# Running streams of a hybrid encoder: cached latents loaded in both layouts, and the two streams of a pair in turn

## The chip, the core and the metric

The kernel runs on one core of a Trainium2 chip. The metric is the device time of one execution in microseconds (us). TensorE (PE) multiplies, VectorE (DVE) and ScalarE (ACT) read its results from PSUM, GpSimd (POOL) works on SBUF alone, and SyncE (SP) issues the DMA transfers, in the order of its own program.

## The reference, cut to what matters

One layer of an encoder with two attention branches side by side, for a prompt of 2048 new tokens and for 8 running streams with 16 new tokens each and 2048 cached positions. The change touches the second branch (latent heads, MLA) of the running streams only:

```python
def mla_attention(q_lat, q_pe, q_pos, ckv, kpe, k_pos):
    mask = chunk_mask(q_pos, k_pos)
    s = (jnp.einsum('bqhc,bkc->bhqk', q_lat, ckv)
         + jnp.einsum('bqhr,bkr->bhqk', q_pe, kpe)).astype(jnp.float32) * MLA_SCALE
    p = masked_softmax(s, mask)
    return jnp.einsum('bhqk,bkc->bqhc', p.astype(ckv.dtype), ckv)
```

`ckv` is the cache of latents, 2048 positions by 256 (fp32) for each stream; `kpe` the positional keys, 2048 by 64. The latents are used twice: contracted over their 256 dimensions for the scores, and over the positions for the output. There are 4 heads, so one stream has 64 rows of queries. The other branch of the running streams is differential attention over cached keys and values of 128 dimensions per head, 4 heads, two softmaxes each.

## The kernel before

The program has four stages: the projections (`_phase_a`, `_phase_a2`), the prompt's attention (`_phase_b`), the running streams (`_sample`), and the output projections with the final norm (`_phase_c`). A scheduler orders the instructions of each engine beforehand, by priorities that follow the program and by its own timeline; on the chip every engine then keeps that order and waits on semaphores.

`_gates` makes tanh factors from a projection of the tokens: for a group of 384 tokens 16 units of 24 matmuls each (L98 to L100, tile `z`), with one weight tile of 512 KB loaded (L380), split on ACT and DVE (L112, L113), and the result stored (L388, L389). The units of groups 3 and 4 may be issued only after the prompt's attention, so they fill PE between the parts of the running streams.

`_sample` works through pairs of streams: `diff_stream(b)`, `mla_streams(b)`, `diff_stream(b + 1)`. A differential stream loads 4 tiles of keys (L734) and 4 of values (L769), 1 MB each; its four heads' scores (L737) go to partitions 0, 32, 64 and 96 of one PSUM bank. `mla_streams` treats two streams at once: stream x writes partitions 64x to 64x + 63 of a bank, its 64 rows. It runs in four chunks of 512 keys. In `chunk(i)` the latents come as [128 positions, 8, 256] (L804, every other chunk, one tile of 1 MB per stream). For each stream PE transposes 2 x 4 blocks of 128 x 128 against the identity (L809), ACT and DVE copy them to a tile `kT` (L816, L814), and then three matmuls follow: two with the latents (L819) and one with the positional keys (L822), where stream x uses rows 64x to 64x + 63 of both operands. The softmax's maximum and exponential are at L716 and L717. After the fourth chunk the weights are scaled on POOL (L846) and transposed (L857), and the output is made in two halves of 1024 keys: eight matmuls for stream 0, then eight for stream 1 (L861), from the same tiles of latents.

All of the big tiles, keys, values, latents and positional keys, come out of one ring (`pk`, tag `k`) of 8 buffers of 1 MB; a load waits until the tile 8 places ahead of it has been read. A second ring `pkt` holds the `kT`. All loads and stores are issued by SP.

`_phase_c` loads the heads' outputs (`ox`, L1175), multiplies them with norm factors on POOL (`r`, L1181), splits them, and multiplies (tile `y`). Its tiles take the memory that the gates' tiles held.

```python
    for b in range(0, NB, 2):
        diff_stream(b)
        mla_streams(b)
        diff_stream(b + 1)
```

Of the kernel before, what the change touches and what calls it, by code (L numbers as in the profile page):

```python
# [11 lines left out]
F32 = mybir.dt.float32  # L12
# [5 lines left out]
PSUM = bass.MemoryType.PSUM  # L18
DRAM = bass.MemoryType.DRAM

P = 128
# [94 lines left out]
def _outer(c, stack):  # L116
    """Pools for the work that fills the engines' gaps: the projections of the gates, later the output projections."""
# [9 lines left out]
def _phase_a(c):  # L127
    nc, tc = c.nc, c.tc
    with (
# [141 lines left out]
        def first_units(us):  # L271
            # the factors of a group follow the sums of the next one
# [14 lines left out]
        def kpe_block():  # L287
            # 64 columns: the weights' two parts side by side, their products added after the load in the next phase
# [61 lines left out]
def _gates(c, prio, g, after, ready):  # L350
    """tanh(m / 2) of m_a and m_b for one group of tokens; ready: the parts of the weights come from memory."""
# [40 lines left out]
def _phase_a2(c):  # L392
    nc, tc = c.nc, c.tc
    with (
# [168 lines left out]
        # the factors of the next group lie between two parts of this one's products  # L563
# [15 lines left out]
def _lam(c, pool, psum):  # L579
    # every partition: exp(sum lq1 lk1) - exp(sum lq2 lk2) + lam_init, negated  # L580
# [12 lines left out]
def _sample_prep(c, temp, psum):  # L593
    """Rotated queries and keys of the new tokens, step by step: rows (s, d); the latent heads' queries in the latent space."""
# [56 lines left out]
    # both halves of the partitions: the streams of a pair take one each  # L651
# [8 lines left out]
    nc.gpsimd.tensor_copy(x.rearrange("p (b h q) -> p b h q", b=NB, h=H), zp.rearrange("p (h b q) -> p b h q", h=H, b=NB))  # L660
# [10 lines left out]
def _sample(c, stack):  # L671
    """Attention of the running streams."""
    nc, tc = c.nc, c.tc
    pkt = stack.enter_context(tc.tile_pool(name="s_kt", bufs=4, reuse_waits="tile"))
    p1 = stack.enter_context(tc.tile_pool(name="s_1", bufs=1, reuse_waits="tile"))
    pk = stack.enter_context(tc.tile_pool(name="s_k", bufs=8, reuse_waits="tile"))
# [21 lines left out]
    # row (h, s, q) of a batch belongs to column (h, q); the second map has weight -lam  # L698
# [9 lines left out]
    def softmax(scores, nm):  # L708
        # scores: PSUM views [128, n]; exponentials (two tiles of 1024 keys, the new keys) and their factors
# [9 lines left out]
        # pm holds the negated maxima  # L719
# [72 lines left out]
    def mla_streams(b):  # L792
# [4 lines left out]
        ks = {}  # L797

        def chunk(i):
            ps = bank("s", f"s{nm}_{i}")  # L800
            for x in range(2):
                if i % 2 == 0:
                    ks[x, i // 2] = big([P, 8, 256], f"k{nm}_{i}_{x}")
                    nc.sync.dma_start(ks[x, i // 2], c.i["cc"][b + x][:, 4 * i : 4 * i + 8, :])  # L804
                kT = pkt.tile([P, 2, 512], F32, tag="kT", name=f"kT{nm}_{i}_{x}", bufs=4)
                for ct in range(2):
                    pk_ = bank("pt", f"kt{nm}_{i}_{x}_{ct}")
                    for j in range(4):
                        nc.tensor.transpose(  # L809
                            pk_[:, j * P : (j + 1) * P],  # L810
                            ks[x, i // 2][:, 4 * (i % 2) + j, ct * P : (ct + 1) * P], c.ident,
                        )
                    if ct:
                        nc.vector.tensor_copy(kT[:, ct], pk_)  # L814
                    else:
                        nc.scalar.copy(kT[:, ct], pk_)  # L816
                out = slice(64 * x, 64 * x + 64)
                for ct in range(2):
                    nc.tensor.matmul(  # L819
                        ps[out, :], QL[:, ct, b + x].rearrange("p h q -> p (h q)"), kT[:, ct], start=(ct == 0), stop=False  # L820
                    )
                nc.tensor.matmul(  # L822
                    ps[out, :], QP[out, b + x].rearrange("p h q -> p (h q)"), kpe[out, i * 512 : (i + 1) * 512],
                    start=False, stop=True,
                )
            return ps

        def fresh():
            ps = bank("pt", f"sn{nm}")
            for x in range(2):  # L830
                bc = slice((b + x) * QS, (b + x + 1) * QS)
                out = slice(64 * x, 64 * x + 64)
                for ct in range(2):
                    nc.tensor.matmul(
                        ps[out, :QS], QL[:, ct, b + x].rearrange("p h q -> p (h q)"), cnT[:, ct, bc], start=(ct == 0), stop=False
                    )
                nc.tensor.matmul(ps[out, :QS], QP[out, b + x].rearrange("p h q -> p (h q)"), kpn[out, bc], start=False, stop=True)
# [5 lines left out]
        for i, e in enumerate(es):  # L843
# [15 lines left out]
            for x in range(2):  # L859
                for kt in range(8):  # L860
                    nc.tensor.matmul(  # L861
                        po[64 * x : 64 * x + 64, :256], at[:, kt * P + 64 * x : kt * P + 64 * x + 64], ks[x, i][:, kt, :],
# [22 lines left out]
    # factors of the sub-norm of the prompt's heads and queries  # L885
# [22 lines left out]
def _phase_b(c):  # L908
    nc, tc = c.nc, c.tc
    GQ = 256  # L910
    with (
# [21 lines left out]
        class Chunks:  # L933
            """Keys [128, 512] or values [128, 4, 128] of one head, loaded 512 keys at a time."""
# [15 lines left out]
        def load_q2(name, src, cols):  # L950
            # src [2 (hi, lo), 64, T]: both halves of the partitions get the same rows
# [411 lines left out]
```

## Time and profile before

| | us |
|---|---|
| runs | 2703.49, 2713.54, 2716.29 |
| median | 2713.54 |
| profiled execution, first to last instruction | 2710.0 |
| PE busy in it | 2569.4 |
| stretch of the running streams, first keys issued to last values issued | 1850.22 to 2267.72 |

The rows are those of one profiled execution of 2710.0 us; no time outside of this span is shown for it, so it is set beside the median of the runs as it stands. A busy PE counts a matmul until its modelled end, which reaches into the next one; what an instruction costs in a row of instructions is therefore read from start to start. An fp32 matmul stands in the trace as two instructions, a transpose as one.

### The profile page before, as it was taken

To read this page: it belongs to the slowest core of one execution; us is meant where nothing else is said; L and a number is where in the kernel's file an instruction comes from. 1 tells how busy PE (TensorE), PEld (TensorE's weight loads), DVE (VectorE), ACT (ScalarE), POOL (GpSimd) and SP (SyncE) were. 2 spreads that over 40 slices of the span, in tenths; PEclk is the share of its full clock that TensorE was granted. 3 is DMA by queue.
4 is the path that set the end of the run, shared out by engine and by line. 5 is a ranking of instruction groups with operands and counts; after the bars stand their busy time and mean duration, and the time that the engine had idled before them with its cause. 6 is when DMAs were issued, how large, how long until landed. Compare 5 with 4: busy or idle time off the path is not lost. (4 is left out here: it accounts for less than half of the span.)

```text
span 2710.0 us, 44913 instructions
## 1 busy us (share of the span) xinstructions
PE 2569.4 (95%) x16308; PEld 2267.0 (84%) x16308; DVE 1436.4 (53%) x3038; ACT 1067.8 (39%) x2682; POOL 703.5 (26%) x944
## 2 busy tenths in 40 slices
PE   7999999999888889999999999999999999999998
PEld 7999999999778878988988888877566575888887
DVE  8236752233666467868776677892323222533334
ACT  5111223212343366766655666772323222311111
POOL 7102220001344233344333334442001001122211
PEclk9999999999889999999999999999999999999999
DMA  5346777322677873474565667317659576534332
GB/s 183 115 147 207 266 255 225 121 68 92 204 243 230 263 218 117 126 202 148 165 194 173 223 203 224 99 54 316 236 220 345 188 291 203 192 117 128 113 108 99
DMA packets 291372, 496.17 MB, mean 183 GB/s; under 512 B 27440, under 2 KB 229200, under 8 KB 280144
## 3 DMA queue, kind: packets, MB, share of 16 engines
q1 hardware_dynamic: 291152, 493.31, 55.5%
q8 instruction: 129, 2.11, 0.3%
q14 instruction: 91, 0.75, 0.1%
HBM read 351.55 MB, written 141.66 MB: 182 GB/s over the span
## 5 line engine op out<-in xcount | busy, mean ns | idle before, releaser
L98 PE MATMUL z<-z_hi,zw 128*128 128x384 f32 (+1 forms) x768 | 262.9, 342 | 26.2 <-ACT zt L388 21.1
L100 PE MATMUL z<-z_hi,zw 128*128 128x384 f32 (+1 forms) x768 | 256.3, 334 | 2.1 <-DMA zw<-wz 1.9
L99 PE MATMUL z<-z_lo,zw 128*128 128x384 f32 (+1 forms) x768 | 257.3, 335 | 0.6 <-POOL z_lo L370 0.6
L977 DVE TENSOR_REDUCE pmd<-sd 128x1 f32<-128x512 f32 (+3 forms) x320 | 189.7, 603 | 58.5 <-PE sd L1051 30.4
L979 ACT ACTIVATE ed<-sd,pmd 128x512 f32<-128x512 f32 (+3 forms) x320 | 200.6, 631 | 47.6 <-DVE pmd L977 35.6
L1078 PE MATMUL sd<-k,q 128*128 128x512 f32 (+2 forms) x640 | 191.0, 384 | 3.5 <-ACT ed L979 1.5
L1018 POOL TENSOR_SCALAR ed<-ed,ad 128x512 f32<-128x512 f32 (+3 forms) x160 | 117.0, 747 | 278.1 <-DVE ad L994 120.5
L98 PEld LDWEIGHTS z<-z_hi,zw 128*128 128x128 f32 x768 | 147.5, 192 | 44.6 <-ACT zt L388 25.4
L99 PEld LDWEIGHTS z<-z_lo,zw 128*128 128x128 f32 x768 | 147.7, 192 | 7.3 <-issue 4.7
L100 PEld LDWEIGHTS z<-z_hi,zw 128*128 128x128 f32 x768 | 146.9, 191 | 6.6 <-DMA zw<-wz 2.3
L1018 POOL TENSOR_SCALAR em<-em,am 128x512 f32<-128x512 f32 (+3 forms) x160 | 104.3, 668 | 157.2 <-DVE am L994 97.1
L98 PE MATMUL y<-o,wh_ab 128*128 128x384 f32 (+1 forms) x384 | 129.0, 336 | 14.9 <-DVE sm L1197 14.9
L113 DVE TENSOR_TENSOR zw<-zs,zw 128x512 fp32r<-128x512 f32 x128 | 89.9, 728 | 92.7 <-ACT zw L112 92.3
L370 POOL TENSOR_TENSOR z_lo<-zx,z_hi 128x384 fp32r<-128x384 f32 (+1 forms) x48 | 48.0, 1026 | 334.6 <-DVE gt L260 260.5
L98 PE MATMUL ps_u<-hi,wh_u 128*128 128x384 f32 (+1 forms) x384 | 126.0, 328 | 6.5 <-ACT wh_u L112 6.5
L100 PE MATMUL y<-o,wl_ab 128*128 128x384 f32 (+1 forms) x384 | 127.8, 333 | 1.4 <-DVE wl_ab L113 1.4
L99 PE MATMUL y<-o,wh_ab 128*128 128x384 f32 (+1 forms) x384 | 128.2, 334 | 0.4 <-DVE o L113 0.4
L1202 ACT ACTIVATE m<-sm 128x384 fp32r<-128x384 f32 (+1 forms) x48 | 24.4, 508 | 259.5 <-POOL sm L1200 259.5
L98 PE MATMUL ps_z<-hi,wh_z 128*128 128x384 f32 (+1 forms) x384 | 125.1, 326 | 1.0 <-ACT wh_z L112 1.0
L99 PE MATMUL ps_u<-lo,wh_u 128*128 128x384 f32 (+1 forms) x384 | 125.7, 327 | 0.0
L99 PE MATMUL ps_z<-lo,wh_z 128*128 128x384 f32 (+1 forms) x384 | 125.0, 325 | 0.0
L100 PE MATMUL ps_u<-hi,wl_u 128*128 128x384 f32 (+1 forms) x384 | 124.9, 327 | 0.0
(365 smaller groups left out, 7567.2 us busy)
## 6 DMA issues: line engine op xcount, KB each, us to landing
zs<-in_wu_dram SPq DMA_DIRECT2D x64, 512.0 KB
zw<-wz SPq DMA_DIRECT2D x64, 512.0 KB
ksd<-in_ckT_dram SPq DMA_DIRECT2D x32, 1024.0 KB
vsd<-in_cv_dram SPq DMA_DIRECT2D x32, 1024.0 KB
q<-Qs SPq DMA_DIRECT2D x128, 128.0 KB
ksm<-in_cc_dram SPq DMA_DIRECT2D x16, 1024.0 KB
smT<-zt SPq DMA_DIRECT2D x80, 192.0 KB
sm<-smT SPq DMA_DIRECT2D x80, 192.0 KB
```

The lines of the kernel that those rows point to most:

```text
L98: nc.tensor.matmul(out, ah, bh, start=(j == 0), stop=False)
L99: nc.tensor.matmul(out, ah, bl, start=False, stop=False)
L100: last = nc.tensor.matmul(out, al, bh, start=False, stop=(j == n - 1))
L113: nc.vector.tensor_tensor(lo, src, hi.bitcast(F32), op=ALU.subtract)
L370: nc.gpsimd.tensor_tensor(lo[:, k], x[:, j], hi[:, k].bitcast(F32), op=ALU.subtract)
L977: nc.vector.tensor_reduce(nm_, ps[:, :w], axis=AX.X, op=ALU.max, negate=True)
L979: nc.scalar.activation(e[:, :w], ps[:, :w], AF.Exp, bias=nm_, accum_out=l[:, s, i : i + 1])
L1018: nc.gpsimd.tensor_scalar(p, p, a[:, 0, j : j + 1], 1.0, op0=ALU.mult, op1=ALU.mult)
L1078: nc.tensor.matmul(ps[:, :n], qs[s][:, j, qc], ks[s].tiles[i][:, :n], start=(j == 0), stop=(j == 1 and not last))
L1202: nc.scalar.mul(z[0], sm[0], 0.5)
```

## The change

Three things are edited. The latents are loaded a second time, with the latent dimension on partitions (`ccT`, a layout of the input like the others), as tiles of 1 MB from the ring; the transposes, the copies and the ring `pkt` go, and the ring `pk` gets 10 buffers. The first layout is loaded later, ahead of the output products. In the scores and the output products the streams 0 and 1 of the pair take turns. For that the rotated queries (`QP`) are laid out over all 128 partitions, with zeros in the half that belongs to the other stream. Comments are dropped.

```diff
@@ _sample_prep
     x = temp("s_QP")
-    nc.gpsimd.tensor_copy(x.rearrange("p (b h q) -> p b h q", b=NB, h=H), zp.rearrange("p (h b q) -> p b h q", h=H, b=NB))
+    nc.gpsimd.memset(x, 0.0)
+    for half in range(2):
+        pr = slice(64 * half, 64 * half + 64)
+        nc.gpsimd.tensor_copy(
+            x.rearrange("p (b h q) -> p b h q", b=NB, h=H)[pr, half::2], zp.rearrange("p (h b q) -> p b h q", h=H, b=NB)[pr, half::2]
+        )
@@ _sample
-    pkt = stack.enter_context(tc.tile_pool(name="s_kt", bufs=4, reuse_waits="tile"))
-    pk = stack.enter_context(tc.tile_pool(name="s_k", bufs=8, reuse_waits="tile"))
+    pk = stack.enter_context(tc.tile_pool(name="s_k", bufs=10, reuse_waits="tile"))
@@ mla_streams: chunk
             ps = bank("s", f"s{nm}_{i}")
+            half = slice(512 * (i % 2), 512 * (i % 2) + 512)
+            if i % 2 == 0:
+                for x in range(2):
+                    kTs[x, i // 2] = big([P, 2, 1024], f"kT{nm}_{i}_{x}")
+                    nc.sync.dma_start(kTs[x, i // 2], c.i["ccT"][b + x][:, :, 512 * i : 512 * i + 1024])
+            for ct in range(2):
+                for x in range(2):
+                    nc.tensor.matmul(
+                        ps[64 * x : 64 * x + 64, :], QL[:, ct, b + x].rearrange("p h q -> p (h q)"),
+                        kTs[x, i // 2][:, ct, half], start=(ct == 0), stop=False,
+                    )
             for x in range(2):
-                if i % 2 == 0:
-                    ks[x, i // 2] = big([P, 8, 256], f"k{nm}_{i}_{x}")
-                    nc.sync.dma_start(ks[x, i // 2], c.i["cc"][b + x][:, 4 * i : 4 * i + 8, :])
-                kT = pkt.tile([P, 2, 512], F32, tag="kT", name=f"kT{nm}_{i}_{x}", bufs=4)
-                for ct in range(2):
-                    pk_ = bank("pt", f"kt{nm}_{i}_{x}_{ct}")
-                    for j in range(4):
-                        nc.tensor.transpose(
-                            pk_[:, j * P : (j + 1) * P],
-                            ks[x, i // 2][:, 4 * (i % 2) + j, ct * P : (ct + 1) * P], c.ident,
-                        )
...
-                out = slice(64 * x, 64 * x + 64)
-                for ct in range(2):
-                    nc.tensor.matmul(
-                        ps[out, :], QL[:, ct, b + x].rearrange("p h q -> p (h q)"), kT[:, ct], start=(ct == 0), stop=False
-                    )
                 nc.tensor.matmul(
-                    ps[out, :], QP[out, b + x].rearrange("p h q -> p (h q)"), kpe[out, i * 512 : (i + 1) * 512],
+                    ps[64 * x : 64 * x + 64, :], QP[:, b + x].rearrange("p h q -> p (h q)"), kpe[:, i * 512 : (i + 1) * 512],
                     start=False, stop=True,
                 )
@@ mla_streams: output products
             for x in range(2):
-                for kt in range(8):
+                ks[x] = big([P, 8, 256], f"k{nm}_{i}_{x}")
+                nc.sync.dma_start(ks[x], c.i["cc"][b + x][:, 8 * i : 8 * i + 8, :])
+            for kt in range(8):
+                for x in range(2):
                     nc.tensor.matmul(
-                        po[64 * x : 64 * x + 64, :256], at[:, kt * P + 64 * x : kt * P + 64 * x + 64], ks[x, i][:, kt, :],
+                        po[64 * x : 64 * x + 64, :256], at[:, kt * P + 64 * x : kt * P + 64 * x + 64], ks[x][:, kt, :],
                         start=(i == 0 and kt == 0), stop=False,
                     )
```

The scheduler makes a new order of all this. On PE, in the first pair's scores, before has transposes (`ktsm`) between the score matmuls (`ssm`, numbered by chunk; the two numbers after `kTsm` are the chunk and the stream, the first two after `ktsm` likewise):

```order
L809 MATMUL ktsm_1_0_0_21876<-ident,ksm_0_0_21836 128x128 x4
L819 MATMUL ssm_0_21835<-kTsm_0_1_21856,sp 64x512
L809 MATMUL ktsm_1_0_1_21882<-ident,ksm_0_0_21836 128x128 x4
L819 MATMUL ssm_0_21835<-kTsm_0_1_21856,sp 64x512
L822 MATMUL ssm_0_21835<-pesm_21826,sp 64x512
L809 MATMUL ktsm_1_1_0_21892<-ident,ksm_0_1_21854 128x128 x4
L819 MATMUL ssm_1_21874<-kTsm_1_0_21875,sp 64x512
L809 MATMUL ktsm_1_1_1_21898<-ident,ksm_0_1_21854 128x128 x4
L819 MATMUL ssm_1_21874<-kTsm_1_0_21875,sp 64x512
L822 MATMUL ssm_1_21874<-pesm_21826,sp 64x512
```

The changed kernel at the same place, where the second number after `kTsm` is the stream (`x2` at the positional keys are the two streams):

```order
L813 MATMUL ssm_0_21834<-kTsm_0_1_21837,sp 64x512
L813 MATMUL ssm_0_21834<-kTsm_0_0_21835,sp 64x512
L813 MATMUL ssm_0_21834<-kTsm_0_1_21837,sp 64x512
L818 MATMUL ssm_0_21834<-pesm_21825,sp 64x512 x2
L813 MATMUL ssm_1_21847<-kTsm_0_1_21837,sp 64x512
L813 MATMUL ssm_1_21847<-kTsm_0_0_21835,sp 64x512
L813 MATMUL ssm_1_21847<-kTsm_0_1_21837,sp 64x512
L818 MATMUL ssm_1_21847<-pesm_21825,sp 64x512 x2
L813 MATMUL ssm_2_21856<-kTsm_2_0_21857,sp 64x512
```

The transposes are gone and the streams are neighbours; the first matmul of stream 0 in chunks 0 and 1 stands earlier, ahead of a whole gate unit, so that three matmuls of stream 1 meet two of stream 0 in each of these chunks.

On SP, the loads of the first pair of latent heads, before:

```order
L795 DMA pesm_21826<-in_cpT_dram 128x2048
L389 DMA smT<-zt_2_24371 128x384
L804 DMA ksm_0_0_21836<-in_cc_dram 128x2048
L380 DMA zs_6_24484<-in_wu_dram 128x1024
L891 DMA rsub<-rsub_24189 128x64
L389 DMA smT<-zt_3_24407 128x384
L804 DMA ksm_0_1_21854<-in_cc_dram 128x2048
L804 DMA ksm_2_0_21910<-in_cc_dram 128x2048
L389 DMA smT<-zt_4_24443 128x384
L804 DMA ksm_2_1_21928<-in_cc_dram 128x2048
L734 DMA ksd_0_22091<-in_ckT_dram 128x2048
```

The second half of the same piece in the changed kernel:

```order
L810 DMA kTsm_2_0_21857<-in_ccT_dram 128x2x1024
L380 DMA zs_6_24099<-in_wu_dram 128x1024
L893 DMA rsub<-rsub_23804 128x64
L389 DMA smT<-zt_3_24022 128x384
L810 DMA kTsm_2_1_21859<-in_ccT_dram 128x2x1024
L860 DMA ksm_0_0_21913<-in_cc_dram 128x2048
L389 DMA smT<-zt_4_24058 128x384
L860 DMA ksm_0_1_21915<-in_cc_dram 128x2048
L860 DMA ksm_1_0_21948<-in_cc_dram 128x2048
L860 DMA ksm_1_1_21950<-in_cc_dram 128x2048
L738 DMA ksd_0_21994<-in_ckT_dram 128x2048
```

Four tiles of the new layout stand ahead of the four of the old one, and the next stream's keys wait behind all eight.

At the end of the gates on PE, the last matmuls of unit 15 of group 4 (`z_15`, weights `zw_4_15`), before:

```order
L98 MATMUL z_15_25426<-z_hi_24844,zw_4_15_25418 128x384
L99 MATMUL z_15_25426<-z_lo_24845,zw_4_15_25418 128x384
L100 MATMUL z_15_25426<-z_hi_24844,zw_4_15_25419 128x384
L819 MATMUL ssm_2_23823<-kTsm_2_0_23826,sp 64x512
L809 MATMUL ktsm_2_1_1_23851<-ident,ksm_2_1_23842 128x128 x4
```

and in the changed kernel:

```order
L98 MATMUL z_15_25041<-z_hi_24459,zw_4_15_25033 128x384
L99 MATMUL z_15_25041<-z_lo_24460,zw_4_15_25033 128x384
L100 MATMUL z_15_25041<-z_hi_24459,zw_4_15_25034 128x384
L98 MATMUL y_0_0_25163<-o_0_25112,wh_ab_25157 128x384
L99 MATMUL y_0_0_25163<-o_0_25113,wh_ab_25157 128x384
```

Before, the gates end amid the last pair's scores; now the streams end first, about 8.5 gate units follow them without anything between but 8 small matmuls (`ov`), and the last stage's `y` comes right after.

## Rows read from the trace of the kernel before

**Rows 1.** The page, busy time, share and instructions of each engine.
```profile
PE 2569.4 (95%) x16308; PEld 2267.0 (84%) x16308; DVE 1436.4 (53%) x3038; ACT 1067.8 (39%) x2682; POOL 703.5 (26%) x944
```
**Rows 2.** Busy time by window: window and length, engines (instructions), PEclk, DMA share, GB/s.
```profile
2060.00:2100.00 40.00, 38.81 (x373) 30.71 (x373) 12.64 (x38) 14.58 (x43) 1.07 (x5) 1.00 0.98 382
2040.00:2100.00 60.00, 55.97 (x475) 43.50 (x468) 18.80 (x52) 22.15 (x60) 4.04 (x10) 1.00 0.92 357
1920.00:2000.00 80.00, 78.36 (x711) 60.79 (x710) 23.19 (x60) 25.59 (x72) 5.85 (x13) 1.00 0.87 329
1850.00:1900.00 50.00, 48.66 (x399) 37.24 (x397) 14.00 (x31) 15.76 (x39) 15.97 (x19) 1.00 1.00 408
1850.00:2300.00 450.00, 436.10 (x3237) 287.64 (x3239) 128.62 (x291) 141.66 (x369) 50.52 (x78) 0.99 0.70 265
```
**Rows 3.** What PE waits for, 1850 to 2300 us: total, times, longest.
```profile
PE z L98 <- ACT zt L388: 7.3, 8, 1.3
```
**Rows 4.** Timeline of SP: first keys and last values of the streams.
```profile
1850.22 1.92 SPq L734 DMA_DIRECT2D ksd<-in_ckT_dram  x4
...
2267.72 0.33 SPq L769 DMA_DIRECT2D vsd<-in_cv_dram  x1
```
**Rows 5.** Windows of the gates (z: PE, PEld, ACT) and of y (PE, PEld, DVE).
```profile
1850.00:2306.70 456.70, 143.75 (x740) 126.00 (x738) 15.06 (x31) 0.99 0.70 263
1850.00:2306.70 456.70, 9.45 (x37) 7.32 (x37) 1.66 (x3) 0.99 0.70 263
```
**Rows 6.** Timeline of PE, one stream's 512 keys: start, length, what.
```profile
1897.10 0.66 PE L809 MATMUL ktsm<-ident,ksm 128*128 128x128 f32 x4
1897.68 1.07 PE L819 MATMUL ssm<-kTsm,sp 128*64 128x512 f32 x2
...
1900.28 1.07 PE L822 MATMUL ssm<-pesm,sp 64*64 64x512 f32 x2
1901.28 0.66 PE L809 MATMUL ktsm<-ident,ksm 128*128 128x128 f32 x4
```
**Rows 7.** Timeline of PE and its weight loads, four heads of a differential stream.
```profile
1926.50 0.16 PEld L737 LDWEIGHTS ssd<-ksd,sp 128*32 128x32 f32 x8 [0.25 <-issue]
1926.50 1.06 PE L737 MATMUL ssd<-ksd,sp 128*32 128x512 f32 x8
...
1927.49 0.45 PE L100 MATMUL z<-z_hi,zw 128*128 128x384 f32 x1
```
**Rows 8.** Timeline of PE, one block of output products.
```profile
1936.08 6.31 PE L861 MATMUL posm<-ksm,atsm 128*64 128x256 f32 x32
1942.33 0.66 PE L857 MATMUL atsm<-ident,esm 128*128 128x128 f32 x4
```
**Rows 9.** Windows of L861 (PE, PEld): one stream, then where the streams meet.
```profile
1936.30:1938.30 2.00, 2.00 (x11) 1.24 (x10) 1.00 0.98 386
1938.72:1939.45 0.73, 0.73 (x9) 0.60 (x8) 1.00 0.42 157
```
**Rows 10.** DMA issues: what, how many, size of one.
```profile
zs<-in_wu_dram SPq DMA_DIRECT2D x64, 512.0 KB
...
ksd<-in_ckT_dram SPq DMA_DIRECT2D x32, 1024.0 KB
...
smT<-zt SPq DMA_DIRECT2D x80, 192.0 KB
...
zx<-in_xT_dram SPq DMA_DIRECT2D x20, 384.0 KB
```
**Rows 11.** What SP waits for, 1850 to 2300 us.
```profile
SPq L1175 <- PE z L100: 15.6, 1, 15.6
```
**Rows 12.** Timeline of the last stage's first load, multiplication and matmul.
```profile
2244.69 0.37 SPq L1175 DMA_DIRECT2D ox<-oT  x1
...
2250.30 1.00 POOL L1181 TENSOR_TENSOR ox<-ox,r 128x384 f32<-128x384 f32 x1 [33.19 <-DMA r<-rsub]
...
2263.51 0.44 PE L98 MATMUL y<-o,wh_ab 128*128 128x384 f32 x1
```

More of the change, by code (lines that the diff above doesn't have):

```diff
@@ L795, in mla_streams @@
         nc.sync.dma_start(kpe, c.i["cpT"][b // 2])
-        ks = {}
+        kTs, ks = {}, {}
         def chunk(i):
             ps = bank("s", f"s{nm}_{i}")
-            for x in range(2):
-                if i % 2 == 0:
-                    ks[x, i // 2] = big([P, 8, 256], f"k{nm}_{i}_{x}")
-                    nc.sync.dma_start(ks[x, i // 2], c.i["cc"][b + x][:, 4 * i : 4 * i + 8, :])
-                kT = pkt.tile([P, 2, 512], F32, tag="kT", name=f"kT{nm}_{i}_{x}", bufs=4)
-                for ct in range(2):
-                    pk_ = bank("pt", f"kt{nm}_{i}_{x}_{ct}")
-                    for j in range(4):
-                        nc.tensor.transpose(
-                            pk_[:, j * P : (j + 1) * P],
-                            ks[x, i // 2][:, 4 * (i % 2) + j, ct * P : (ct + 1) * P], c.ident,
-                        )
[L813 to L816, printed above, removed]
-                out = slice(64 * x, 64 * x + 64)
-                for ct in range(2):
-                    nc.tensor.matmul(
-                        ps[out, :], QL[:, ct, b + x].rearrange("p h q -> p (h q)"), kT[:, ct], start=(ct == 0), stop=False
-                    )
+            half = slice(512 * (i % 2), 512 * (i % 2) + 512)
[9 more added lines that the diff above has]
+                    )
+            for x in range(2):
                 nc.tensor.matmul(
-                    ps[out, :], QP[out, b + x].rearrange("p h q -> p (h q)"), kpe[out, i * 512 : (i + 1) * 512],
+                    ps[64 * x : 64 * x + 64, :], QP[:, b + x].rearrange("p h q -> p (h q)"), kpe[:, i * 512 : (i + 1) * 512],
                     start=False, stop=True,
@@ L829, in fresh, with each @@
             ps = bank("pt", f"sn{nm}")
[L830 to L833, printed above, removed]
+            def each(lhs, rhs, ct):
+                for x in range(2):
+                    bc = slice((b + x) * QS, (b + x + 1) * QS)
                     nc.tensor.matmul(
-                        ps[out, :QS], QL[:, ct, b + x].rearrange("p h q -> p (h q)"), cnT[:, ct, bc], start=(ct == 0), stop=False
+                        ps[64 * x : 64 * x + 64, :QS], lhs(x).rearrange("p h q -> p (h q)"), rhs[:, bc], start=(ct == 0), stop=(ct == 2)
                     )
-                nc.tensor.matmul(ps[out, :QS], QP[out, b + x].rearrange("p h q -> p (h q)"), kpn[out, bc], start=False, stop=True)
+            for ct in range(2):
+                each(lambda x: QL[:, ct, b + x], cnT[:, ct], ct)
+            each(lambda x: QP[:, b + x], kpn, 2)
             return ps[:, :QS]
@@ L859, in mla_streams @@
             for x in range(2):
-                for kt in range(8):
+                ks[x] = big([P, 8, 256], f"k{nm}_{i}_{x}")
+                nc.sync.dma_start(ks[x], c.i["cc"][b + x][:, 8 * i : 8 * i + 8, :])
+            for kt in range(8):
+                for x in range(2):
                     nc.tensor.matmul(
-                        po[64 * x : 64 * x + 64, :256], at[:, kt * P + 64 * x : kt * P + 64 * x + 64], ks[x, i][:, kt, :],
+                        po[64 * x : 64 * x + 64, :256], at[:, kt * P + 64 * x : kt * P + 64 * x + 64], ks[x][:, kt, :],
                         start=(i == 0 and kt == 0), stop=False,
@@ L1314, in layout @@
     a["cc"] = cc.reshape(NB, 16, P, 256).transpose(0, 2, 1, 3)
+    a["ccT"] = cc.transpose(0, 2, 1).reshape(NB, 2, P, PAST).transpose(0, 2, 1, 3)
     a["cpT"] = inp["cache_mla_kpe"][0].transpose(0, 2, 1).reshape(NB // 2, P, PAST)
```

## The prediction

> **What bounds the kernel now.** I read the page first: PE is busy 95% of a span of 2710.0 us [rows 1], so time is won where PE gets less to do or waits less, and nowhere else. The change lies in one stage, the running streams, so next I read the busy times by window: from 1850 to 2300 us PE is busy 436.1 of 450 us at a granted clock of 0.99, DVE 129, ACT 142, the DMA engines 0.70 of the time [rows 2]. The list of what PE waits for in this stretch is headed by 7.3 us behind ACT's tanh of the gates and holds no load [rows 3]. So PE is the bound here, its program order is the schedule, and an instruction taken off PE shortens the stage as long as nothing else becomes late. The stage's ends: the first keys are issued at 1850.22 and the last values at 2267.72 [rows 4]; gate products of groups 3 and 4, 143.8 us of PE for 740 matmuls, lie between its parts, and 9.5 us of the last stage's products (y) are done before 2306.70, from where that stage has PE for itself [rows 5]. Without y the stage costs 456.5 - 9.5 = 447 us. That is the number the change works on.
>
> **What is removed: the transposes.** One stream's 512 keys take from 1897.10 to 1901.28, 4.18 us [rows 6]: four transposes, 0.58 us; a score matmul, 1.01; four transposes, 0.58; a score matmul, 1.01; the positional one, 1.00. With 4 pairs, 4 chunks and 2 streams that is 32 x 4.18 = 134 us. The copies out of PSUM (32 on ACT, 32 on DVE) go too; I cost them at nothing, since those engines are busy a third of the stretch [rows 2] and PE is not waiting for them [rows 3].
>
> **What is made concurrent: the scores.** In after's order the matmuls of the two streams are neighbours; they write partitions 0 to 63 and 64 to 127, other columns of the array. Before shows what neighbours on other columns cost: the four heads of a differential stream, 8 instructions with four different weights and moving operands, take from 1926.50 to 1927.49, 0.99 us [rows 7], as long as one score matmul of 2 instructions alone. So I count units of 1.0 us, in which each half of the columns does one matmul. Perfect alternation needs 3 units a chunk, 48 in all. The new order isn't perfect: for two pairs stream 0's first matmul of two or four chunks runs alone, then come three for stream 1 against two. Following its rows I count 16, 16, 13 and 13 units for the four pairs, 58 us. The positional matmul now uses all 128 rows, half of them zeros; this is free, as 64 rows took the 1.00 us that 128 rows took [rows 6]. Scores and transposes: 134 - 58 = 76 us.
>
> **The products with the latents** come by blocks of 32 instructions, today eight matmuls of one stream and then eight of the other, 1936.08 to 1942.33, 6.25 us [rows 8]. Only where the streams meet do they overlap: 8 weight loads start in 0.73 us there, 0.09 each, against 10 in 2.00 us, 0.20 each, within one stream [rows 9]. Alternating throughout, I take 32 x 0.11 = 3.5 us, nearest to half of 6.25. Eight blocks: 8 x 2.75 = 22 us. PE loses 76 + 22 = **98 us** in all.
>
> [...]
>
> **What is added: loads.** The latents come a second time, 16 transfers of 1024 KB. Counting the queue's new order from the first keys to the last values: 100 transfers of 1024 KB, 20 of gate weights of 512, 20 gate results of 192, 4 of 384 [rows 10], 120.8 MB. In before 84 of the large ones, 27 gate weights and 31 results went in the same stretch, over 417 us [rows 4]; there was time. Now there may not be. The engines moved 408 GB/s over 50 us at share 1.00, 382 over 40 us at 0.98, 357 over 60 us at 0.92, and 329 over 80 us at 0.87, where some loads waited for a buffer [rows 2]. So the last values land 296, 316, 338 or 367 us after 1850. Two more buffers (10 for 8) deepen the look-ahead, but the pair of mla needs nine of them at once, and SP's queue is in order: a load that waits for a buffer holds the gate weights behind it.
>
> [...]
>
> **What is moved: the gates, and the last stage's start.** The new order places fewer gate units between the parts: 8.5 of them stand behind the last product of the streams, at 143.8 x 24 / 740 = 4.66 us [rows 5], so 39.6 us of PE alone after the streams. In before the gates end just ahead of 2244.7 with 60 us of streams still to come, and these cover the start of the last stage: its first load waits for the last gate matmul (15.6 us) [rows 11], is issued at 2244.69, POOL has the factors at 2250.30, and y begins at 2263.51 [rows 12]. In after y stands right behind the last gate matmul, and that load still waits for it, so PE will stand idle there. Bounds: 5.6 us (until POOL starts) and 18.8 us (to y, with other work ahead on ACT and PE). I take 12, the middle, since the chain goes on over a multiplication and a split but without the competitors. POOL's clearing and its second copy of the rotated queries cost nothing: they belong to the preparation, steps ahead of the stage, on an engine that is busy 26% of the span [rows 1].
>
> **The sum.** Loads at 382 GB/s: 316 + 1 (last values) + 39.6 + 12 = 369, which is 78 less than 447. At 357: 338 + 52.6 = 391, 56 less. By PE alone: 98 - 12 = 86 less. PE and the loads are nearly even, so each will wait for the other now and then; I take the middle of the two load figures, **67 us less**: 2710 - 67 = 2643 us of span. The median of the runs, 2713.5, stands 3.5 above this span, so I forecast **2646 us**.
>
> **The rivals.**
> - PE stays the bound and the loads hide: 86 us less, 2627; with units of 0.9 us and the short start at most 98, 2616. For it: before's waits hold no load. Against it: 408 GB/s was seen only when every buffer was free.
> - The loads bind harder, at the 329 GB/s of a stretch with buffer waits: 367 + 52.6 = 420, 27 less, 2687. For it: 0.70 was the mean share in before, because buffers weren't free.
> [...]
> - Slower than before: the ring of ten buffers and SP's order keep the transfers at the stage's mean of today, 265 GB/s [rows 2]. Then 120.8 MB take 456 us, and 456 + 52.6 = 509 is 62 more, 2775. This decides from 447 - 52.6 = 394 us on, below 306 GB/s. Against it: today's mean is low because PE held the buffers, and it will give them back sooner.
> - Between these, rates of 296 to 317 GB/s would leave the time within 0.5%.
>
> **How the numbers follow.** 0.5% is 13.6 us, about what a measurement of this kernel can tell from no change. Chances: forecast 0.46, PE-bound 0.18, loads at about 329 0.18, no overlap 0.05, no change 0.07, slower 0.06. Faster is 0.46 + 0.18 + 0.18 + 0.05 = 0.87. The range runs from 2616 (PE-bound, short start) to 2690 (slow loads, no overlap) and leaves out the last two.
>
> **What would show it.** The score rows should stand in pairs some ns apart and a chunk take 3 to 4 us, the latent blocks 3.5 us, the transposes be gone. PE's waits in the stage should now name loads (keys, latents), with a DMA share near 0.9 until the last values; if they name none, PE was the bound. Between the last gate matmul and the first y there should be a gap of about 12 us. The prediction is wrong if the stage's PE time falls by less than 80 us, if the gap is absent, or if the last values are issued before 2130 or after 2230.

## The result and the profile after

The changed kernel takes 2671.2 us (median of 4 runs, 2667.0 to 2676.1) against 2709.0 for the kernel before beside it: ratio 0.9856, 95% interval 0.9827 to 0.9885, or 38 us less. The forecast was 67 less, 2646 (range 2616 to 2690). So the sign held and the size was a little over half. The two profiled spans differ by 45 us, 2710.0 to 2665.1, but 9 of these lie ahead of the change: the last product of the stage before (`om`) starts at 1843.0 in the one and 1834.3 in the other. From there to the end it is 867.0 and 830.8, 36 us less, which agrees with the medians. Where two traces are set side by side below, I count from that product.

Timeline of PE in the changed kernel: the scores of one 512-key chunk for both streams, then one block of output products (start, length, what).

```profile
2132.03 1.94 PE L813 MATMUL ssm<-kTsm,sp 128*64 128x512 f32 x8
2133.80 1.03 PE L818 MATMUL ssm<-pesm,sp 128*64 128x512 f32 x4
2134.66 1.89 PE L813 MATMUL ssm<-kTsm,sp 128*64 128x512 f32 x8
...
2152.26 3.67 PE L863 MATMUL posm<-ksm,atsm 128*64 128x256 f32 x32
2155.86 1.09 PE L856 MATMUL atsm<-ident,esm 128*128 128x128 f32 x8
```

A chunk takes 2.63 us for two streams, where before each stream took 4.18 [rows 6]; a block takes 3.60 to the next row, before 6.25 [rows 8]. These are the two gains that the forecast counted on, and they are there.

Windows of the changed kernel: window and length, busy time of PE, PEld, DVE, ACT, POOL (instructions), granted clock, DMA share, GB/s.

```profile
1850.00:2150.00 300.00, 277.20 (x2421) 191.81 (x2420) 83.61 (x207) 96.47 (x269) 36.21 (x59) 0.92 0.97 381
```

and the same stretch before:

```profile
1850.00:2150.00 300.00, 292.53 (x2157) 192.44 (x2159) 86.90 (x191) 95.53 (x245) 34.47 (x53) 1.00 0.70 270
```

Two things are new. The DMA share has gone from 0.70 to 0.97, at 381 GB/s, the upper of the two rates that the forecast took (382 and 357). And the granted clock has gone from 1.00 to 0.92, which the forecast didn't have at all. What PE waits for in the changed kernel, 1850 to 2245 us (total, times, longest):

```profile
PE atsd L763 <- DVE Wsd L758: 11.9, 4, 5.4
PE z L98 <- ACT zt L388: 11.3, 11, 1.4
PE y L98 <- ACT wh_ab L112: 9.9, 1, 9.9
PE atsm L856 <- POOL esm L845: 6.3, 3, 3.2
```

No line of it is a load, nor are the four shorter ones that follow. PE waits for the end of a softmax (`Wsd`, `esm`), for the gates' only PSUM bank (`zt`), and once 9.9 us for the first weights of the last stage. By the forecast's own sign ("if they name none, PE was the bound") the loads did not bind. They land early, too. SP issues a stream's four tiles of keys (2002.2, 2007.0, 2007.4 and 2008.9), and PE first reads them much later:

```profile
2002.21 0.33 SPq L738 DMA_DIRECT2D ksd<-in_ckT_dram  x1
...
2008.88 0.42 SPq L738 DMA_DIRECT2D ksd<-in_ckT_dram  x1
...
2028.09 1.02 PE L741 MATMUL ssd<-ksd,sp 128*32 128x512 f32 x2
```

By my estimate, which counts the bytes of the DMA records in the order of issue, the first of them had landed by about 2009, 19 us ahead of its use. Over the 64 tiles of keys and values the same estimate gives a lead of about 18 us in the median and 2 at least. So the DMA engines were nearly always busy (share 0.97), but with data that PE didn't need yet.

The pauses have a second price. PE's timeline around the longest pause in the streams, a later pause, and windows around both and at the start of the last stage:

```profile
2037.82 0.34 PE L100 MATMUL z<-z_hi,zw 128*128 128x384 f32 x1
2043.56 2.82 PE L763 MATMUL atsd<-Wsd,esd 128*128 128x64 f32 x12 [5.39 <-DVE Wsd L758]
...
2071.67 2.00 PE L856 MATMUL atsm<-ident,esm 128*128 128x128 f32 x12 [2.63 <-POOL esm L845]
```

```profile
2030.00:2040.00 10.00, 8.16 (x58) 4.25 (x46) 4.22 (x9) 4.58 (x13) 1.14 (x3) 1.00 0.96 375
2040.00:2050.00 10.00, 6.44 (x30) 6.44 (x31) 3.55 (x10) 2.32 (x8) 3.45 (x4) 0.65 1.02 411
2044.00:2049.00 5.00, 5.00 (x26) 5.00 (x25) 0.15 (x1) 0.77 (x3) 0.00 (x0) 0.50 1.01 410
2050.00:2060.00 10.00, 10.00 (x162) 6.69 (x163) 2.58 (x5) 2.37 (x7) 1.92 (x5) 0.83 0.69 245
2070.00:2080.00 10.00, 8.29 (x64) 4.57 (x66) 4.49 (x10) 5.97 (x12) 3.08 (x6) 1.00 1.03 421
2240.00:2250.00 10.00, 5.94 (x12) 3.21 (x12) 6.69 (x6) 3.95 (x6) 2.19 (x2) 0.50 0.94 253
```

The granted clock is 1.00 up to 2040 and 0.65 and 0.83 in the next 20 us; from 2044 to 2049 it is 0.50, which I call the lower level. Behind the 9.9 us pause at the start of the last stage it is 0.50 too. It doesn't fall behind each pause: 2.6 us from 2069.0 on left it at 1.00, while 1.4 us ahead of `atsd`, from 2015.3 on, were followed by a granted clock of 0.70 from 2020 to 2030. In these rows the falls come behind pauses, but why one pause is followed by a fall and another not, no run here shows.

So I split PE's time from `om` to the end of streams and gates, in windows of about 4 us, into **work** (busy time times granted clock), **clock** (busy time times one minus it, what the lower level costs) and **idle**. That work goes with the granted clock is an estimate from rows like these: in a row of 128x384 matmuls each starts 0.17 us behind the one ahead of it at 1.00 (2230.38 to 2230.55) and 0.32 us at 0.50 (2242.59 to 2242.91).

| kernel | length | work | clock | idle | ratio to before |
|---|---|---|---|---|---|
| before | 459.2 | 440.7 | 3.1 | 15.4 | 1 |
| changed | 396.6 | 339.2 | 21.7 | 35.6 | 0.9856 |
| products alternate only (e1) | 438.4 | 420.5 | 2.9 | 15.0 | 0.9932 |
| no alternation (e2) | 438.4 | 377.6 | 21.6 | 39.2 | 1.0046 |
| 12 loads fewer (e3) | 369.8 | 331.7 | 7.9 | 30.2 | 0.9789 |
| pools of the last stage (e4) | 395.5 | 341.4 | 17.8 | 36.2 | 0.9777 |
| ring of 8 (e10) | 378.9 | 336.2 | 18.3 | 24.5 | 0.9798 |
| 24 matmuls added (e11) | 394.1 | 354.7 | 5.8 | 33.5 | 0.9867 |

PE's work falls by 101.5 us, of which some 9 are `y` products that lay inside the streams before and don't now: 92 net, where the forecast had 98. Of these, 20.2 come back as idle time and 18.6 as the lower clock. The rest goes at the seam to the last stage: the pause of 9.9 us, and the first 37 `y` matmuls, which spread over 20.6 us (2240.8 to 2261.4) for 9.45 us of work [rows 5]. In sum 92 - 20 - 19 - 10 - 11 = 32, against 36 measured. The 4 us left are what the kernel before had at this place: there 4.8 us lay between the end of the last product (2302.2) and its 38th `y` (2307.0), with the last `ov` and five `y`.

What the idle time consists of is in PE's list of waits over the same stretches. Waits ahead of the softmaxes' transposes (`atsd`, `atsm`, `otsd`, `otsm`) make 2.6 us before and 21.0 in the changed kernel, waits ahead of gate matmuls 10.3 and 13.9. So 18 of the 20 us are waits for softmaxes.

### The profile page after: what moved, and what is told of

The parts are those of the page before. It is cut to its first block, busy times and chain, and to the rows that moved or that the text cites. A ratio compares the mean times of both kernels' runs of the same rounds, so it can differ in the third digit from the quotient of the medians.

```text
span 2665.1 us, 44335 instructions
## 1 busy us (share of the span) xinstructions
PE 2489.6 (93%) x16052; PEld 2239.2 (84%) x16052; DVE 1416.6 (53%) x3006; ACT 1050.3 (39%) x2650; POOL 706.5 (27%) x946
```

## The experiments

Each is one edit, or several joined where it says so. Times are medians of 4 runs (e2: 7, e8: 1); ratios are to the kernel before on the same chip, whose median was 2708 to 2713.

**e1: the products alternate, nothing else.** The kernel before with

```
-            for x in range(2):
-                for kt in range(8):
+            for kt in range(8):
+                for x in range(2):
```

> The kernel before, with one edit: the products of the weights with the latents alternate the two streams, matmul by matmul; transposes, loads and scores stay. Its program order keeps all gate units between the streams. My theory: in the kernel before PE is the bound and a block of 32 falls from 6.25 to the 3.67 us that the changed kernel shows, so 8 x 2.6 = 21 us come off: about 2688, ratio 0.992. Rival, that the two streams do not overlap by themselves (the gain of the block comes from elsewhere): blocks stay at 6.25 and the time at 2709. Second rival, a hidden wait takes the place: blocks fall, the time does not.

Measured 2690.2 us, ratio 0.9932 (0.9910 to 0.9953), 18 us less by the ratio. Timeline of PE, one block:

```profile
1939.39 3.67 PE L861 MATMUL posm<-ksm,atsm 128*64 128x256 f32 x32
1943.00 0.66 PE L857 MATMUL atsm<-ident,esm 128*128 128x128 f32 x4
```

The block is as short as in the changed kernel, work falls by 20.2 us, and idle and clock stay (table). Here a gain on PE arrives in the time almost in full: the kernel before was bound by PE, as the forecast said, and the streams overlap by order alone (3.61 us a block for 6.25). The two rivals fall.

**e2: the second load, but no alternation.** The changed kernel with stream 0's matmuls ahead of stream 1's, in `chunk` (`for x` outside `for ct`, the positional one behind them) and in the products (the edit of e1 undone).

> The changed kernel without the alternation: stream 0's matmuls, then stream 1's, in the scores and in the products; the second load of the latents and the missing transposes stay. My theory: a chunk's scores go from 2.63 to about 6 us (16 chunks, +54) and a block of products from 3.67 to 6.25 (8 blocks, +21), so PE becomes the bound of the streams, and with 9.8 instead of 8.5 gate units behind the last product the time is some 45 to 60 us over the changed kernel: 2715 to 2730, no better than the kernel before. Rival, the streams are bound by the loads and PE has slack: at most +25, below 2700. Rival, the overlap does not depend on the order in the program: no difference, 2671.

Measured 2722.4, ratio 1.0046 (1.0031 to 1.0062): slower than before. The time was as expected, its parts were not. Timeline of PE, one chunk:

```profile
2076.82 1.94 PE L813 MATMUL ssm<-kTsm,sp 128*64 128x512 f32 x6
2078.54 0.59 PE L817 MATMUL ssm<-pesm,sp 128*64 128x512 f32 x1
2078.59 0.59 PE L813 MATMUL ssm<-kTsm,sp 128*64 128x512 f32 x1
...
2080.31 1.94 PE L813 MATMUL ssm<-kTsm,sp 128*64 128x512 f32 x6
```

A chunk takes 3.49 us here, not 6: where one stream's last matmuls meet the other's first, these start 0.05 us apart. With the transposes gone the streams meet twice a chunk, so a part of the overlap comes unasked. Over all chunks the scores cost 25 us more than alternating (76.3 against 51.5, start to start, 5 of them a pause that falls among the scores), the products 21. The whole is the lesson: PE has 63 us less work than before (54 without `y`), and the kernel is 12 us slower. Idle time (24 more), clock (18 more) and the seam (22: a pause of 10.2, and 21.4 for the first 37 `y`) come to 64, more than the 54.

**e3: 12 of the 16 added loads left out.** In `chunk` one tile of latents a pair, for both streams and all chunks:

```
-            if i % 2 == 0:
-                for x in range(2):
-                    kTs[x, i // 2] = big(...)
+            if i == 0:
+                z = big([P, 2, 1024], f"kT{nm}_{i}")
+                nc.sync.dma_start(z, c.i["ccT"][b][:, :, 0:1024])
+                for x in range(2):
+                    kTs[x, 0] = kTs[x, 1] = z
```

> The changed kernel with 12 of its 16 added loads left out: the scores of the latent heads of a pair all read the first 1024 latents of its first stream, so those scores are computed from other data. PE's instructions stay, 12.6 MB of loads go. My theory: the loads at 381 GB/s bind the streams, so these end up to 12.6 / 0.381 = 33 us earlier, unless PE stops it first (its work in the streams without waits is 305 us of the 331, so at 26 us): the last product at 2150 to 2160 instead of 2181. Its order leaves 10.5 gate units behind instead of 8.5, 2 x 5.9 = 12 us, so the time is 10 to 20 us less: 2651 to 2661. Rival, PE's waits for the softmax chain are the bound and the loads hide: the last product moves only by the 8 us of the two gate units, and the time is 2670 to 2680.

Measured 2653.4, ratio 0.9789 (0.9760 to 0.9818), the last product at 2149.7: the numbers of my theory. (Counted from `om` the last product comes 38 us earlier than in the changed kernel, more than the 33 us that the loads could give by it.) But the rows don't bear it out. PE's waits, 1850 to 2150 us:

```profile
PE z L98 <- ACT zt L388: 5.6, 6, 1.2
PE atsm L857 <- POOL esm L846: 2.5, 1, 2.5
PE atsd L763 <- DVE Wsd L758: 2.4, 1, 2.4
```

What went is not a wait for loads, since there was none, but 13 us of waiting for softmaxes (18.2 to 4.9), and with it 14 us of lower clock (table). The scheduler orders the program by its own times, and with fewer loads it put the gate products elsewhere. So e3 can't tell the loads from the order; which of the two freed those waits stays open. That the loads are not the limit rests on the waits and on the early landings; e10 fits it. Against it stands that the queue ran at 387 GB/s here, no slower than with all the loads.

**e4: the last stage's first tiles on other memory.** The pools of `_phase_c` in another order: `d_m` and a new `d_wo` for the output weights first, so that they lie where the gates' tiles were, then `d_t`, `d_x`, `d_o`, `d_v`, `d_w`.

> The changed kernel with the pools of the last stage allocated in another order: the tiles needed first (factors, attention output, first weights) lie where the streams' tiles were, the ones needed late (output weights, later results) where the gates' tiles were, so the first loads need not wait for the last gate matmul. My theory: the gap of 10.3 us between the last gate matmul and the first y and the slow start after it (the first 37 y matmuls took 20.6 us at a granted clock of 0.5 to 0.7, for 9.5 us of work) both go: 15 to 20 us less, 2651 to 2656. Rival, the start is held by other work (the split of the first weights on ACT and DVE, POOL's multiplication), so only part of the gap goes: 0 to 8 less.

Measured 2647.5, ratio 0.9777 (0.9756 to 0.9797), 24 us below the changed kernel and the fastest of all. Timeline of PE where the gates meet `y`, and a window there:

```profile
2219.70 0.34 PE L100 MATMUL z<-z_hi,zw 128*128 128x384 f32 x1
2219.87 0.34 PE L98 MATMUL y<-o,wh_ab 128*128 128x384 f32 x1
```

```profile
2240.00:2250.00 10.00, 9.31 (x47) 8.15 (x47) 5.92 (x8) 3.50 (x6) 1.93 (x1) 1.00 0.65 216
```

The first `y` stands amid the gates, 22 us earlier counted from `om`, no pause ahead of it remains, and the clock stays at 1.00 where it was 0.50. The pause of 9.9 us had cost some 21 with what followed it. The load of the heads' outputs (`ox`) is issued at 2187.7, right behind the streams' last `ov`, and no longer behind the last gate matmul; the gate units cover what follows it.

**e5: a second PSUM bank for the gates of groups 3 and 4** (every other unit uses a new bank `z2`; `pt` has 2 instead of 3).

> The changed kernel with a second PSUM bank for the gate units of groups 3 and 4, taken from the softmax's banks for transposes (2 instead of 3). In the tail behind the streams a unit takes 5.90 us, of which PE waits 1.44 for ACT to empty the only bank; my forecast had 4.66 a unit. My theory: the wait goes, a unit behind the streams takes about 4.2 us, and 9.25 units behind (its order has 222 matmuls there, 18 more) take 39 instead of 50 us: 8 to 12 less, 2659 to 2663. Rival, the wait passes on to the weights of the gates (their load and split on ACT and DVE): units stay near 5.9 and the time is 2671 or, with 0.75 units more behind, 2675. Second rival, two banks are too few for the streams' softmax: streams end later than 2181 by more than the tail wins.

Measured 2673.7, ratio 0.9852 (0.9834 to 0.9870): no gain. The units behind the streams do take 4.42 us (40.9 us for 9.25) instead of 5.90, but the last product of the streams comes 8 us later after `om`. That is the sign of the second rival, but its reason isn't shown: PE's list holds no wait for a bank of transposes. By the same split as above, idle time falls by 8 us (27.5) and the lower clock takes 7 more (29.1), so what the bank wins the clock takes back.

**e6: gate units between the pairs.** `_gates` yields after each unit, and `_sample` takes 9, 9, 9 and 5 units behind the four pairs.

> The changed kernel with the gate units emitted between the pairs of streams (9, 9, 9 and 5 behind the four pairs) instead of behind all of them, so that the scheduler fits more of them in: its order leaves 6 units behind the last product instead of 8.5. My theory: inside the streams the loads bind and PE waits 26 us, so 2.5 units more cost nothing there, and the tail loses 2.5 x 5.9 = 15 us: 2654 to 2660. Rival, PE binds the streams as much as the loads: the units moved only save their 1.44 us of waiting, 4 us, 2667. Second rival, the gates' earlier place holds up the streams' matmuls, buffers come free later and the last values are issued after 2160: the time grows.

Measured 2671.8, ratio 0.9839 (0.9818 to 0.9861): within 5 us of the changed kernel, and not the 2654 to 2660 of the theory. Counted from `om`, the gates end 11.6 us earlier, the streams 5 later. **e9** joins it with e4:

> The two edits that won something, together: gate units emitted between the pairs (9, 9, 9, 5; 6 units behind the last product) and the last stage's pools in the other order. From the end of the stage before, the first alone brought the end 7.5 us forward in its profile, the second 23.5. My theory: they add up nearly, since one shortens the tail and the other joins it to the last stage: 5 to 10 us below the second alone, 2637 to 2643. Rival, that PE has no slack left in the streams (it waits 25 us there and runs some 20 us' worth of work at the lower clock level): the spread gives nothing more, 2645 to 2652.

Measured 2649.0, ratio 0.9768 (0.9748 to 0.9787), the same as e4: the rival. The 2.5 units that are moved in push the last product out by 11 us, counted from `om`, and idle time in the stretch stays (33.5 us against 36.2 in e4): they don't fall into the pauses.

**e7: e4 to e6 together**, units 12, 12, 8, 0.

> All three together: gate units emitted between the pairs (12, 12, 8, 0), the second bank for them, and the last stage's pools in the other order. Its order leaves no gate unit behind the last product. PE's work from 1850 on is then 305 us of streams and some 36 for the 8.5 units that came from the tail, 341 if it never waits, while the loads need 331 with the last softmax. My theory: y begins at 2190 to 2205 without a gap instead of 2241 with one, 2605 to 2620. Rival, the gates ahead of the streams delay the freeing of the buffers, the loads stall at first and are missed later: last values issued after 2175, time 2630 to 2645.

Measured 2678.0, ratio 0.9867 (0.9850 to 0.9884). Both expectations miss: the last values are issued at 2167, not after 2175, but `y` begins at 2247. No gate unit is left behind the streams, so the last stage's start has nothing to cover it. PE waits 11.5 us for the first weights again, and 26.2 us go to the clock. SP and PE there:

```profile
2236.57 0.57 SPq L1186 DMA_DIRECT2D ox<-oT  x1
2247.28 0.69 PE L98 MATMUL y<-o,wh_ab 128*128 128x384 f32 x1 [11.49 <-ACT wh_ab L112]
```

With the new pools `ox` comes behind the streams instead of the gates, and here the streams end last (`ov` starts at 2235.5, their last store is issued at 2236.1). From `ox` to the first `y` some 10 us pass, as in the changed kernel (2230.75 to 2240.84). The softmax waits are 20.5 us here, although all 32 gate units lie inside the streams again, as before the change.

**e8: positional scores on 64 rows**, `QP[64 * x : 64 * x + 64, b + x]` and `kpe` alike.

> The changed kernel with the positional score matmuls on 64 rows each, as in the kernel before (stream x on rows 64x to 64x + 63), instead of 128 rows of which half are zeros; the alternation and the order stay. My forecast called the padding free. Theory: the positional rows keep 0.286 us start to start and the time stays at 2671, within 8 us. Rival, that rows of their own let the two streams overlap better (or the halves disturb each other): the 64 instructions move by more than 2 us in sum.

One run, 2682.6. The positional matmuls take 16.1 us in sum instead of 18.3, so they move by 2.2, just past the 2 us of the rival; those with the latents take 39.6 instead of 33.2. The span is 15.7 longer, but 10 of these come ahead of `om`; one run can't settle the rest. Taking the padding out at least wins nothing that shows.

**e10: a ring of 8.** `bufs=8` for `s_k`.

> The changed kernel with a ring of 8 tiles for the loads, as before, instead of 10. Its order leaves 4 gate units behind the last product instead of 8.5. Theory: with two tiles fewer loads wait for buffers more often, the mean rate falls from 378 to 340 to 355 GB/s and the last values are issued 340 us or more after the end of the stage before, instead of 322; what the shorter tail wins (4.5 x 5.9 = 26 us) is given back: 2662 to 2685. Rival, the depth does not matter, because the DMA queue itself binds: last values at 318 to 328 us, the tail 26 us shorter, 2645 to 2655.

Measured 2659.2, ratio 0.9798 (0.9775 to 0.9822), 12 below the changed kernel, between the ranges of the theory and of the rival. The last values are issued 328 us after `om` instead of 322. So the loads of the streams end 6 us later, not the 18 or more of the theory: less look-ahead harms little, which fits data that lie ready 18 us early. PE idles 11 us less, in an order that leaves 4 units behind instead of 8.5; what else of the order helps wasn't tried. **e12** joins it with e4:

> The changed kernel with both edits that its own runs favoured: a ring of 8 tiles instead of 10 (12 us below the changed kernel by itself) and the last stage's pools in the other order (24 below). Its order leaves 2.4 gate units behind the last product. Theory: with the depth of the ring without effect on the loads, what is won is the order of the gate units, and the two edits add up in part: 2630 to 2642. Rival, as with the gates emitted between the pairs, a shorter tail gives nothing once the last stage joins it without a gap, since PE has the same work and the same lost clock in the streams: 2644 to 2652.

Measured 2650.1, ratio 0.9787 (0.9762 to 0.9812): the rival's time, but not its reason, because here the last stage does not join without a gap. SP and PE at the seam:

```profile
2208.95 0.40 SPq L1178 DMA_DIRECT2D ox<-oT  x1
2218.61 0.69 PE L98 MATMUL y<-o,wh_ab 128*128 128x384 f32 x1 [5.61 <-ACT wh_ab L112]
```

Streams and gates end 18 us earlier after `om` than in e4 (377.8 us against 395.5), but 2.4 gate units are too few to cover the 10 us from `ox` to the first `y`: PE waits 5.6 us, and the first 37 `y` spread over 22.8 us at a granted clock of 0.56. With the new pools the pause ahead of `y` is 0 us with 8.5 units behind the last product (e4), 0.6 with 6 (e9), 5.6 with 2.4 (e12) and 11.5 with none (e7). So moving gate units forward and joining the last stage early draw on the same units.

**e11: useless work in the pauses.** Ahead of the differential stream's transposes

```
+        idle = bank("pt", f"idle{nm}")
+        for _ in range(3):
+            nc.tensor.matmul(idle, c.ident, es[1][:, 512:1024], start=True, stop=True)
```

> The changed kernel with 24 matmuls added whose result nobody reads: three in each differential stream (identity by the last chunk's exponentials, 128 x 512, 1.0 us each), which stand before the transposes of the weights, where PE waits for the softmax chain. Its order leaves 8 gate units behind. My theory: the granted clock falls because PE stood idle just before, so filling part of the waits keeps it up: the wait for the pair weights falls from 11.9 us to under 6, the work lost to the lower level (busy time times one minus the granted clock, in steps of 5 us over the 330 us of streams) from 21.8 us to under 12, and of the 24 us added most come back: 2665 to 2682. Rival, the lower level has to do with the loads or the load on the chip, not with idle time: 17 to 26 us lost as in the other variants, and the time 15 to 25 us up, 2686 to 2696.

Measured 2677.8, ratio 0.9867 (0.9845 to 0.9889), not to be told from the changed kernel. Window:

```profile
1850.00:2150.00 300.00, 278.59 (x2490) 188.02 (x2490) 81.68 (x209) 95.62 (x269) 39.85 (x66) 0.98 0.98 391
```

The wait for `Wsd` is gone from the list, the granted clock is 0.98 instead of 0.92, and the lower level costs 5.8 us instead of 21.7, with the DMA share as high as before. 24 us of matmuls were added, the other matmuls of the stretch take 24 us less, start to start, 16 of them by the clock, and streams and gates end 2.5 us earlier. So the loads by themselves didn't bring the clock down. Nor did the sum of PE's idle time: it hardly fell (33.5 us against 35.6). What is gone are the four waits ahead of `atsd`, and in the changed kernel the lower level had followed each of these, for 7 to 14 us. Waits ahead of `atsm` remain, 5.1 and 3.5 us long; behind the first the granted clock is 0.85 from 2068 to 2078, behind the second it stays at 1.00.

## Why the forecast came out as it did

- **Transposes and scores, -76.** Right: start to start, transposes and scores went from 130.1 us to 51.5, 79 less. A chunk at its best took 2.63 us, less than the 3 to 4 expected.
- **Products with the latents, -22.** Right: 50.9 to 30.3, 21 less, and e1 shows it by itself. That the two streams would not overlap has a chance of 0.05 in the forecast and a part in the end of its range, 2690; no run shows it. In e1 the block's form is 128*64, so both streams use all 128 rows and one half of the columns each, and by turns they took 3.61 us where one behind the other took 6.25.
- **Loads at 357 to 382 GB/s, 316 to 338 us.** The size was right: first keys at 1842.1, last values at 2156.4 (the second of the two below), 314 us, at 381 GB/s.

```profile
1842.05 1.92 SPq L738 DMA_DIRECT2D ksd<-in_ckT_dram  x4
...
2155.95 0.80 SPq L773 DMA_DIRECT2D vsd<-in_cv_dram  x2
```

  The role was wrong. I took the middle between two load figures as the limit, and expected PE's waits to name loads; none did. By the forecast's own sign PE was the bound, the first rival ("PE stays the bound and the loads hide", 2627). What set the rate isn't settled. For PE, which gives the buffers back, speak SP's waits (from 1850 to 2150, 26.4 us of them behind `ssm` and 23.3 behind `posd`) and e2, where PE had more to do and the rate was 351. For the queue speaks e3, where it stayed at 387 with fewer loads and the last values came 37 us earlier after `om`.
- **"PE by itself, 86 less".** This step failed by what it left out. It took PE's waits in the streams as they were before. Idle time went from 15.4 to 35.6 us, 18 of it in waits for softmaxes, and the clock fell behind pauses for another 18.6. My reading is that the transposes had also been cover: without them, the next matmul in the order stands closer behind the softmax that it needs. With transposes the softmax waits are 2.6 us (before and e1), without them 7.4 to 23.3, and e7 shows that it isn't for want of gate units. But the order that the scheduler made counts as well (7.4 in e3, 13.9 in e10), and no run changes the transposes alone, so this stays argued.
- **8.5 gate units at 4.66 us, 39.6.** Mis-sized: 50.1 us (2180.8 to 2230.9), 5.90 a unit. The 4.66 was busy time, without the wait for the only bank, which other matmuls mostly filled in the kernel before; alone, a unit shows it in full:

```profile
2196.04 0.34 PE L100 MATMUL z<-z_hi,zw 128*128 128x384 f32 x1
2197.82 0.44 PE L98 MATMUL z<-z_hi,zw 128*128 128x384 f32 x1 [1.44 <-ACT zt L388]
```

- **A gap of 12 us at the last stage's start.** It was 9.95:

```profile
2230.55 0.34 PE L100 MATMUL z<-z_hi,zw 128*128 128x384 f32 x1
2240.84 0.69 PE L98 MATMUL y<-o,wh_ab 128*128 128x384 f32 x1 [9.95 <-ACT wh_ab L112]
```

  But the first `y` lasts 0.69 us and not 0.44 as the first of a gate unit does, and the 37 first ones lost 11 us more, to the clock and to waits for the split of the heads' outputs (`o`, 7.7 us). e4 gives gap and slow start back together.
- **Look-ahead of ten buffers.** Next to no effect on the loads: with eight the last values come 6 us later, and the kernel is 12 us faster in the order that goes with it (e10).

The total landed inside the range, 25 us above the forecast, but partly by luck: the forecast gave 19 us away to loads (86 less by PE alone, 67 in the end) that no wait shows, and had nothing for the idle time (20), the lower clock (19) and the slow start of `y` (11). None of its signs of being wrong came: PE's work fell by 92 us net, the gap was there, and the last values were issued at 2156. The kernel before also ran 4.5 us faster beside the changed one than the 2713.5 that the forecast started from. The edit does take the work off PE; more than half of it is lost again in pauses, in the clock behind them, and at the seam.

## What to carry to other kernels

Work that is taken off the bounding engine may also have covered something: count, at each dependent step behind it, what is left between producer and consumer. Price the pauses on PE as a range, since the granted clock fell to 0.50 behind some of them here and stayed at 1.00 behind others: beside 33 to 36 us of idle time the lower clock took between 6 (e11) and 23 us (e9). A DMA share near 1 alone doesn't show that loads are the bound (0.97 here, with no load among PE's waits); look whether PE's waits name one, and how long data lie before their first use. And look at the seam to the next stage: here, placing its first tiles on memory that comes free earlier gave 24 us, two thirds of what the change itself gave, as long as enough gate units stood behind the streams to cover the 10 us from its first load to its first matmul.

## What the runs showed that I had not expected

- Short pauses on PE cost about as much again in clock here: 20.2 us more idle time, 18.6 us more at the lower level. In the kernel before, where no wait from 1850 to 2150 is longer than 1.5 us, the clock there was 1.00; behind its one wait of 2.1 us, at 2268.7, it was 0.83 over 10 us. The sum of the pauses didn't decide it: 24 us of matmuls nobody reads, put ahead of `atsd`, left 33.5 us of idle time, took 16 us off the clock's cost, and cost no measurable time (e11).
- Matmuls of the two column halves started 0.05 us apart even where the program has one stream's matmuls behind the other's (e2), with all 128 rows in use by both.
- The order of two loops alone was worth 18 us (e1). With the scores' order, and the transposes between them gone, it was worth 51 (e2, 1.0046 against 0.9856).
